# A two-layer attention and retention trunk: the order of the first supertile's queue, rotation and retention, the place of the output weights' squares, and the order of products in the first projection tiles

## The chip, the core and the metric

The kernel runs on one core of a Trainium2 chip. The core has five engines that each work through an instruction queue of their own, in order: TensorE (PE in the profile; its weight loads are listed apart as PEld), VectorE (DVE), ScalarE (ACT), GpSimd (POOL) and SyncE (SP), which issues the DMA transfers here. An instruction that needs another engine's result waits on a semaphore, and everything behind it in the same queue waits too. The metric is the device time of one execution, in microseconds (us).

## What is computed

Two layers, each `x <- x + W_out(concat[A(h) * silu(g_A), B(h) * silu(g_B)])` with `h = RMSNorm(x)`, then a last RMSNorm. There are 2048 tokens, a model width of 1024, 8 attention heads of 64 and 4 retention heads of 128. The core of the reference:

```python
proj = rms_norm(x, norm_gain[layer]) @ w_in
aq, ak, av, ag, rq, rk, rv, rg = jnp.split(proj, cuts, axis=-1)

# A: softmax attention over the own chunk of 64 and the 8 chunks before it
scores = einsum(qc, kb) * dh**-0.5 + rel_bias[clip(dist, -256, 256) + 256]
ya = softmax(where(valid, scores, -1e30)) @ vb

# B: retention; q and k are rotated by position, cos and sin of position * inv_freq
rotated = concat([t1 * c - t2 * s, t1 * s + t2 * c])
att     = einsum(qc, kc) * intra_decay
o_intra = att @ vc
state   = state * chunk_decay + kv          # from chunk to chunk
o_inter = einsum(qc, q_decay, state)
yr      = rms_norm(o_intra + o_inter)

x = x + concat([ya * silu(ag), yr * silu(rg)]) @ w_out
```

Everything is float32. The kernel gets there with fp16 matmuls: each factor is written as an upper half (`h`) and a rest (`l`), and a product is the sum of three matmuls, upper by upper, upper by rest and rest by upper.

## The kernel before, in words

**Tiling.** The kernel works by head pairs: in each layer `s` = 0 to 3 counts four pairs of attention heads with one retention head each, and each head pair runs over four supertiles `n` = 0 to 3 of 512 tokens. The normalized, transposed input of a supertile is `hTh` (upper) and `hTl` (rest), 8 blocks (`kt`) of 128 input channels, each with 512 tokens on the free axis. Tokens come in tiles of 128, numbered 0 to 15; supertile 0 holds tokens' tiles 0 to 3, supertile 1 holds 4 to 7.

**Projections.** `dense_T` (line 608) makes four tiles of a supertile, channels by tokens, each in 24 matmuls (8 blocks times 3 products): `j` = 0 is the attention's q, 1 its k, 2 the retention's q, 3 its k. The general loop stands at line 730; the very first supertile has its own, by token quarters, at line 712. `dense_V` (line 738) makes four tiles `a` = 0 to 3, tokens by channels, of 24 matmuls each at line 750: the columns are attention values, retention values and the gates. In both loops the three products of one block follow each other, block by block. The PSUM tiles come from a pool of two buffers (`psD`), so a tile can begin only when the one two before it has been read out. For V that reading ends on DVE in `rests` (lines 762 to 768), which is put off by one round; its three instructions write the rest of `v`, the rest of `rv` and the gate `gt`.

**Rounds.** A round is 8 matmuls of a projection. `run` advances the projection of the next supertile by a round, lets `attention` (line 783) of the supertile before take one of its 24 steps, runs what was put off with `later(k, f)` (f is issued k rounds on), and pulls a share of the background steps, which were handed over with `push(generator, steps)`. So TensorE's queue holds projection matmuls with attention and retention work between them. The instruction order within an engine is this order of issue where the code says so by hand, and the scheduler's elsewhere.

**Attention units.** A supertile has 8 units (4 tiles of 128 tokens, 2 heads), one in 3 rounds: scores S (lines 798, 799), bias and maximum on DVE (802), exp on ACT (805), the split into upper and rest (807 on ACT, 808 on POOL), a transposing DMA (810), the product with v (818 to 820) and its scaling on DVE (824 to 833).

**Retention.** `retention` (line 863) runs beside it: per token tile two steps, 8 in all. The first makes the scores r (products, line 853), their masking (872) and their split (`upper_of`, line 857, on ACT, and `rest_of`, line 861, on DVE, into a tile called dT in the profile). The second makes the output and the next state. DVE updates the state at lines 893 to 901, and lines 905 to 912 scale the output. The 8 steps are taken in rounds 0, 5, 6, 11, 12, 17, 18 and 23 of 24.

**Rotation.** For `j` = 2 and 3 `evacuate` (line 631) copies the tile out of PSUM as `raw`, `swap` exchanges its halves with two DMAs (line 666, into `swp`), and then follow, each some rounds on: `turn` (three POOL operations, lines 670 to 672, with the cosine and sine tables), `upper` (ACT, 675), `lower` (DVE, 678), for q `third` (ACT, 681) and for k `tokens` (a transposing DMA, 685).

**The first supertile.** Up to the end of its V tiles SP's queue has an order written by hand (`sp_order`), and the other engines get their work from a list of named steps. `x...4` to `x...7` are the steps of the next four token tiles: `sq` square, `rs` root, `mul` gain and scale, `hi` and `lo` the upper half and rest of the rows (token tile 7's stand on ACT and DVE), `dma` the two transposing DMAs into `hTh` and `hTl` (line 236). `bt` makes a bias tile from a table in memory: a POOL memset (580), a DMA (577), an ACT operation (581). `u` is one step of `tables` (line 83), which makes the cosine and sine tables of supertile 1 from its positions: it loads positions (`xa`, line 89), casts them on DVE (99), and goes on with DVE and ACT operations (93 to 124). The list that runs beside the last rounds is

```python
push(rounds(["xhi4 xrs5 xrs6", "xlo4 xmul5 xrs7", "xdma4 xhi5 xmul6 bt", "xlo5 xhi6 u", "xdma5 xlo6 xmul7",
             "xdma6 xhi7", "xlo7", "xdma7 u", "u u bt", "u u bt", "u u", "u u bt"]), 12)
```

`norms_from_input` (line 1148) does the same for later token tiles and loads their x itself; tiles 8 to 11 go into four spaces called `late`.

**Weights.** `convert` splits a head pair's weights into upper and rest: the rest of V's (`wlV`) is written on DVE (line 333). `prep_Omax` (line 492) takes the sum of squares of all of a layer's output weights, as their common scale needs it: 8 loads of 512 KB, 8 ACT squares (line 309) with DVE additions, and a sum over partitions. It is handed over as 13 steps in supertile 0 of `s` = 2, just before that supertile's V tiles. The bias tiles of a new head pair (`bt`) are made in supertile 0 as well.

## Time and profile before

| | |
|---|---|
| median of 3 runs | 2113.38 us (2111.25 to 2114.31) |
| the profiled execution's own time | 2117.65 us |
| its span | 2115.9 us |
| its mean granted TensorE clock | 0.987 |
| instructions | 39456 |
| HBM read, written | 123.26 MB, 41.98 MB |

The profile comes from one execution, and its span runs from the first to the last instruction that it recorded. A row of a group of instructions names the engine, the source line and the operands by the program's names (output<-inputs), the number, busy time and mean duration, and then the idle time of that engine just ahead of them with what ended it. A timeline row has the start (us from the span's beginning), the duration, the engine, the instruction, and in brackets the wait ahead of it with its releaser. Matmuls overlap in the records: their durations are longer than the distance between their starts. SPq rows are issues of DMAs, not their transfers.

### The profile page before, as it was taken

To read this page: it belongs to the slowest core of one execution; us is meant where nothing else is said; L and a number is where in the kernel's file an instruction comes from. 1 tells how busy PE (TensorE), PEld (TensorE's weight loads), DVE (VectorE), ACT (ScalarE), POOL (GpSimd) and SP (SyncE) were. 2 spreads that over 40 slices of the span, in tenths; PEclk is the share of its full clock that TensorE was granted. 3 is DMA by queue.
4 is the path that set the end of the run, shared out by engine and by line. 5 is a ranking of instruction groups with operands and counts; after the bars stand their busy time and mean duration, and the time that the engine had idled before them with its cause. 6 is when DMAs were issued, how large, how long until landed. Compare 5 with 4: busy or idle time off the path is not lost.

```text
span 2115.9 us, 39456 instructions
## 1 busy us (share of the span) xinstructions
PE 2010.4 (95%) x14014; PEld 1052.1 (50%) x14014; DVE 1253.8 (59%) x3839; ACT 1139.1 (54%) x2522; POOL 679.5 (32%) x701
## 2 busy tenths in 40 slices
PE   6778999999999999988999999999999999999998
PEld 4334555555455555544444555555545555554543
DVE  7677566655565655566653556555656566556643
ACT  7455665556655654555444546554665465446432
POOL 1233333433343433321002343434333433433200
PEclk9899999999999999999999999999999999999999
DMA  8767675558665764699875556555685567548874
GB/s 247 165 119 164 137 164 113 115 110 191 148 113 111 159 158 99 132 197 259 206 187 115 121 103 140 123 124 103 149 186 119 101 137 169 123 101 182 217 193 127
DMA packets 645701, 313.63 MB, mean 148 GB/s; under 512 B 459232, under 2 KB 602080, under 8 KB 645504
## 3 DMA queue, kind: packets, MB, share of 16 engines
q1 hardware_dynamic: 645504, 311.12, 66.5%
q8 instruction: 109, 1.79, 0.4%
q14 instruction: 88, 0.72, 0.1%
HBM read 123.26 MB, written 41.98 MB: 78 GB/s over the span
## 4 chain that ended last, share of the span: by engine, by line
PE 47%; DMA 3%; ACT 2%; DVE 2%; issue 1%; POOL 1%; SPq 1%; POOLq 0%; DVEq 0%; ACTq 0%
PE dT L730 14%; PE dV L750 14%; PE dO L1090 12%; DMA pT<-pq 2%; PE r L853 2%; PE S L799 1%; PE S L798 1%; PE o L818 1%; PE o L819 1%; PE o L820 1%; DVE sc L802 1%; ACT sc L805 0%; ACT pq L807 0%; DMA yhy<-rhy 0%; DMA bias<-toep 0%
## 5 line engine op out<-in xcount | busy, mean ns | idle before, releaser
L808 POOL TENSOR_TENSOR pq<-sc,pq 128x640 f16<-128x640 f32 (+4 forms) x256 | 319.9, 1250 | 930.1 <-ACT pq L807 562.5
L805 ACT ACTIVATE sc<-sc,mq,cT 128x640 f32<-128x640 f32 (+4 forms) x256 | 218.5, 853 | 653.8 <-DVE rl L824 330.4
L730 PE MATMUL dT<-hTh,whT 128*128 128x512 f16 x1008 | 386.0, 383 | 11.9 <-DVE rv L766 7.8
L750 PE MATMUL dV<-wlV,hTh 128*128 128x512 f16 x1024 | 389.1, 380 | 6.9 <-DVE wlV L333 6.9
L750 PE MATMUL dV<-whV,hTh 128*128 128x512 f16 x1024 | 389.3, 380 | 6.2 <-DVE gt L768 6.1
L730 PE MATMUL dT<-hTl,whT 128*128 128x512 f16 x1008 | 386.2, 383 | 4.6 <-DMA hTl<-hTl 2.9
L750 PE MATMUL dV<-whV,hTl 128*128 128x512 f16 x1024 | 389.0, 380 | 0.0
L730 PE MATMUL dT<-hTh,wlT 128*128 128x512 f16 x1008 | 385.7, 383 | 0.0
L730 PEld LDWEIGHTS <-whT 128*128 128x128 f16 x2016 | 195.9, 99 | 236.7 <-issue 20.4
L750 PEld LDWEIGHTS <-hTh 128*128 128x128 f16 x2048 | 197.7, 98 | 223.9 <-DVE gt L768 9.1
L802 DVE CUSTOM_DVE_ANT_0 sc<-S,bias 128x640 f32<-128x640 f32 (+4 forms) x256 | 188.8, 737 | 154.7 <-PE S L799 150.8
L1090 PE MATMUL dO<-whO,yhy 128*128 128x512 f16 x512 | 194.8, 381 | 1.9 <-DMA yhy<-rhy 1.9
L1090 PE MATMUL dO<-whO,yly 128*128 128x512 f16 x512 | 194.6, 380 | 0.8 <-DMA yly<-rly 0.8
L1090 PE MATMUL dO<-wlO,yhy 128*128 128x512 f16 x512 | 194.6, 380 | 0.0
L807 ACT ACTIVATE pq<-sc 128x640 f16<-128x640 f32 (+4 forms) x256 | 171.5, 670 | 11.1 <-DMA pT<-pq 3.0
L1090 PEld LDWEIGHTS <-yhy 128*128 128x128 f16 x1024 | 99.9, 98 | 117.2 <-DMA yhy<-rhy 2.6
L750 PEld LDWEIGHTS <-hTl 128*128 128x128 f16 x1024 | 100.3, 98 | 115.8 <-issue 9.9
L730 PEld LDWEIGHTS <-wlT 128*128 128x128 f16 x1008 | 99.3, 98 | 106.4 <-issue 4.3
L818 PE MATMUL o<-v,pT 128*128 128x65 f16 x1120 | 129.8, 193 | 15.6 <-DMA pT<-pq 15.5
L798 PE MATMUL S<-k,q 128*128 128x128 f16 (+3 forms) x592 | 142.3, 267 | 0.7 <-DVE mq L802 0.7
L818 PEld LDWEIGHTS <-pT 128*128 128x128 f16 x1120 | 105.7, 97 | 51.0 <-DMA pT<-pq 21.5
L819 PE MATMUL o<-v,pT 128*128 128x64 f16 x1120 | 130.0, 195 | 0.0
(350 smaller groups left out, 3499.3 us busy)
## 6 DMA issues: line engine op xcount, KB each, us to landing
q<-qq SPq DMA_DIRECT2D x128, 128.0 KB, 2.5
yyy<-y_d SPq DMA_DIRECT2D x32, 512.0 KB, 4.6
stT<-in_w_in_dram SPq DMA_DIRECT2D x27, 512.0 KB, 4.8
stV<-in_w_in_dram SPq DMA_DIRECT2D x26, 512.0 KB, 4.4
k<-kk SPq DMA_DIRECT2D x128, 64.0 KB, 2.1
swp<-rot SPq DMA_DIRECT2D x64, 128.0 KB, 2.6
tabc<-tab SPq DMA_DIRECT2D x32, 256.0 KB, 2.7
tabs<-tab SPq DMA_DIRECT2D x32, 256.0 KB, 3.1
```

The costliest lines, as they stand in the source:

```text
L730: pe.matmul(ps, w_[:, j, kt, :], h_[:, kt, :], start=(m == 0), stop=(m == 23))
L750: pe.matmul(ps, h_[:, kt, a * P:(a + 1) * P], w_[:, kt, :], start=(m == 0), stop=(m == 23))
L798: pe.matmul(o, st.q[:, hx, 0, cs], k_, start=True, stop=False)
L799: pe.matmul(o, st.q[:, hx, 1, cs], k_, start=False, stop=True)
L802: dve.tensor_tensor_reduce(out=v, in0=S[:, 0:w], in1=g.bias[hx][:, 640 - w:640], scale=1.0, scalar=-3.0e38, op0=ALU.add, op1=ALU.max, accu ...
L805: act.activation(v, v, AF.Exp, bias=m[:, 0:1], scale=g.c[:, 0:1])
L807: act.activation(pq[:, 0:w], v, AF.Copy)
L808: pool.tensor_tensor(pq[:, w:2 * w], v, pq[:, 0:w], op=ALU.subtract)
L818: pe.matmul(o[:, 0:65], u.p[:, b, :], v_[:, 0:65], start=(b == 0), stop=False)
L819: pe.matmul(o[:, 0:64], u.p[:, b, :], v_[:, 65:129], start=False, stop=False)
L853: pe.matmul(out_, w_, m_, start=(i == 0), stop=(i + 1 == len(pairs)))
L1090: pe.matmul(ps, h_[:, kt, :], w_[:, kt, :], start=(m == 0), stop=(m == 23))
```

## The change

Five edits:

1. `in_order`: in `dense_T` for `j` = 0 and in `dense_V` for `a` = 0 the 24 products are issued term by term (8 blocks of the first product, 8 of the second, 8 of the third). In the other tiles they stay block by block; in both, the order of the three products within a block or of the terms is changed (`hTl` last for T, `wlV`'s product last for V).
2. The first supertile's rotation: for q (`j` = 2) `upper`, `lower` and `third` go from rounds 6, 7, 8 after the evacuation to 11, 12, 13; for k (`j` = 3) `swap` goes from 5 to 9 rounds, while `turn`, `upper`, `lower` and `tokens` stand 3, 5, 6 and 7 rounds after it, as before.
3. The first supertile's retention takes its 8 steps in rounds 5, 10, 10, 14, 14, 18, 18 and 23.
4. The loads of x for token tiles 8 to 11 are steps `x8` of the hand-written list, behind `xdma7`, and `norms_from_input` leaves them out there; three of the `u` steps leave that list (7 in place of 10) and are pushed in the next supertile with the rest.
5. `prep_Omax` is handed over in supertile 2 of `s` = 2 in place of supertile 0, in both layers.

```diff
 
+    def in_order(apart, terms):
+
+        return [(kt, w) for w in terms for kt in range(KT)] if apart else [(kt, w) for kt in range(KT) for w in terms]
+
     def dense_T(l, s, n, g, st):
...
 
-                    d = 4 if j == 2 and first else 3
-                    later(d, turn)
-                    later(d + 2 if first else d + 3, upper)
-                    later(d + 3 if first else d + 4, lower)
-                    if j == 2:
-                        later(d + 4 if first else d + 6, third)
-                    if j == 3:
-                        later(7 if first else 11, tokens)
+                    if not first:
+                        plan = {3: turn, 6: upper, 7: lower, **({9: third} if j == 2 else {11: tokens})}
+                    elif j == 2:
+                        plan = {4: turn, 11: upper, 12: lower, 13: third}
+                    else:
+                        plan = {3: turn, 5: upper, 6: lower, 7: tokens}
+                    for k_, fn in plan.items():
+                        later(k_, fn)
 
...
                     st.rk = rot
-                    later(5 if first else 2, swap)
+                    later(9 if first else 2, swap)
 
...
             m = 0
-            for kt in range(KT):
-                for (w_, h_) in ((g.h, hh), (g.h, hl), (g.l, hh)):
-                    pe.matmul(ps, w_[:, j, kt, :], h_[:, kt, :], start=(m == 0), stop=(m == 23))
-                    m += 1
-                    if m in (8, 16) or (m == 24 and first):
-                        yield
+            for kt, (w_, h_) in in_order(j == 0, ((g.h, hh), (g.l, hh), (g.h, hl))):
+                pe.matmul(ps, w_[:, j, kt, :], h_[:, kt, :], start=(m == 0), stop=(m == 23))
+                m += 1
+                if m in (8, 16) or (m == 24 and first):
+                    yield
             evacuate(j, ps)
...
             m = 0
-            for kt in range(KT):
-                for (w_, h_) in ((g.vh, hh), (g.vl, hh), (g.vh, hl)):
-                    pe.matmul(ps, h_[:, kt, a * P:(a + 1) * P], w_[:, kt, :], start=(m == 0), stop=(m == 23))
-                    m += 1
-                    if m in (8, 16):
-                        yield
+            for kt, (w_, h_) in in_order(a == 0, ((g.vh, hh), (g.vh, hl), (g.vl, hh))):
+                pe.matmul(ps, h_[:, kt, a * P:(a + 1) * P], w_[:, kt, :], start=(m == 0), stop=(m == 23))
+                m += 1
+                if m in (8, 16):
+                    yield
             rv = gp.tile([P, 3, P], F16, tag="rv", name=f"rv{nm}_{a}")
...
         ret = retention(l, s, n, g, st)
+        rounds_ret = (5, 10, 10, 14, 14, 18, 18, 23) if (l, s, n) == (0, 0, 0) else [6 * a + b for a in range(4) for b in (0, 5)]
         for i, (a, hx) in enumerate(units):
...
             u = qk(a, hx)
-            if i % 2 == 0:
-                next(ret, None)
-            yield
-            yield
-            if i % 2 == 1:
-                next(ret, None)
-            pipe.append(lambda u=u: pv(u))
-            yield
+            for r in range(3 * i, 3 * i + 3):
+                for _ in range(rounds_ret.count(r)):
+                    next(ret, None)
+                if r % 3 == 2:
+                    pipe.append(lambda u=u: pv(u))
+                yield
 
...
             u.x = spaces[k] if spaces else w4.tile([P, D], F32, tag="w4", name=f"xin{u.t}")
-            sp.dma_start(u.x, x[u.t * P:(u.t + 1) * P, :])
+            if not spaces:
+                sp.dma_start(u.x, x[u.t * P:(u.t + 1) * P, :])
 
...
     t1 = tables(1, [xs0[1][:, i * 256:(i + 1) * 256] for i in range(4)])
-    steps = {"d": lambda: go_on(d0), "t": lambda: go_on(t0), "u": lambda: go_on(t1), "r": lambda: go_on(rl_),
+    x8 = (sp.dma_start(late[t - 8], x[t * P:(t + 1) * P, :]) for t in range(8, 12))
+    steps = {"x8": lambda: go_on(x8), "d": lambda: go_on(d0), "t": lambda: go_on(t0), "u": lambda: go_on(t1), "r": lambda: go_on(rl_),
              "Tu": T_un, "Vu": V_un, "bs": lambda: go_on(bs0), "bt": lambda: go_on(bt0)}
...
     g00.vdone = 4
-    push(rounds(["xhi4 xrs5 xrs6", "xlo4 xmul5 xrs7", "xdma4 xhi5 xmul6 bt", "xlo5 xhi6 u", "xdma5 xlo6 xmul7", "xdma6 xhi7",
-                 "xlo7", "xdma7 u", "u u bt", "u u bt", "u u", "u u bt"]), 12)
+    push(rounds(["xhi4 xrs5 xrs6", "xlo4 xmul5 xrs7", "xdma4 xhi5 xmul6 bt", "xlo5 xhi6", "xdma5 xlo6 xmul7", "xdma6 xhi7",
+                 "xlo7", "xdma7 x8", "u x8 bt", "u u x8 bt", "u u x8", "u u bt"]), 12)
     att = [None]
...
                     if n == 1:
-                        push(t1, TAB_STEPS - 10)
+                        push(t1, TAB_STEPS - 7)
                     push(norms_from_input(range(4 * n + 4, 4 * n + 8), late[0:4] if n == 1 else None,
...
                     push(wout_first(l, go, us), 10)
-                if n == 0 and s == 2:
+                if n == 2 and s == 2:
                     push(prep_Omax(l, go), 13)
```

## The prediction

> **What bounds the kernel now.** The page's first two parts come first: which engine is full, and where it is not.
>
> ```profile
> span 2115.9 us, 39456 instructions
> PE 2010.4 (95%) x14014; PEld 1052.1 (50%) x14014; DVE 1253.8 (59%) x3839; ACT 1139.1 (54%) x2522; POOL 679.5 (32%) x701
> PE   6778999999999999988999999999999999999998
> ```
>
> TensorE is busy for 2010.4 of 2115.9 us, and the holes stand in the first four slices (212 us). No matmul is added or removed, so the change can only touch the 105.5 us in which PE idles, and the half-speed stretches behind long idles. The view of waits, for PE alone, says what ended these idles (total, times, longest).
>
> ```profile
> PE r L853 <- DVE dT L861: 15.6, 10, 5.3
> PE r L853 <- ACT dT L857: 9.2, 3, 4.5
> PE dT L730 <- DVE rv L766: 7.8, 1, 7.8
> PE dV L750 <- DVE wlV L333: 6.9, 5, 1.6
> PE dT L730 <- DMA hTl<-hTl: 2.9, 1, 2.9
> PE dT L730 <- DMA hTl<-rln: 1.6, 2, 0.9
> ```
>
> Those six rows make 44 us, and each belongs to an edit. I take them by edit, the plainest first.
>
> **First tiles' products, term by term.** For V the first tile of four now multiplies whV by hTh eight times, whV by hTl eight times, and only then reads wlV; before, wlV was read by the second matmul.
>
> ```profile
> 506.00 0.38 PE L750 MATMUL dV<-wlV,hTh 128*128 128x512 f16 x1 [1.34 <-DVE wlV L333]
> 506.21 0.38 PE L750 MATMUL dV<-whV,hTl 128*128 128x512 f16 x1
> 506.43 0.38 PE L750 MATMUL dV<-whV,hTh 128*128 128x512 f16 x1
> ```
>
> Matmuls start 0.215 us apart. Sixteen before the first use of wlV instead of one add 15 x 0.215 = 3.2 us of cover, more than the longest of the five waits (1.6). The 6.9 us go, unless PE, 1.3 us earlier, meets the next wait sooner; the five reach from 1.3 to 1.6, so I leave 0.3 for that: **6.6**, bounds 4 (half of them come back) and 6.9.
>
> For the T tiles the same reordering puts hTl behind 16 matmuls on hTh. The two waits on hTl from the rln rows, 0.9 at the longest, are covered: **1.6**, bounds 0 and 3 (some half-clocked matmuls go with them).
>
> The Trainium skill, "TensorE: Matmul & The Clock Gate", section "Step-by-step: what each phase is for", speaks against such an order: weights are kept apart from the matmul so that one load can serve several matmuls, and the old order put the same weights twice in a row. In this trace nothing was kept: the page counts 14014 loads for 14014 matmuls, so by the row the order costs nothing; by the rule some of the T and V tiles' pairs would lose a load.
>
> **Squares of the output weights, two supertiles on.** `prep_Omax` leaves supertile 0 of the third head pair (s = 2) for supertile 2, in both layers: 8 loads of 512 KB, 8 squares with their accumulator reads, the additions, one matmul. Here are what the two places look like, ACT's squares, and the wait with its surroundings (ACT, then SP, then PE).
>
> ```profile
> 509.00:532.00 23.00, 22.70 (x163) 11.61 (x160) 11.51 (x40) 18.44 (x42) 11.69 (x11) 1.00 1.00 240
> 615.00:638.00 23.00, 23.00 (x173) 12.45 (x172) 15.00 (x46) 13.64 (x35) 11.33 (x12) 1.00 0.42 92
> L309 ACT ACTIVATE stO0m<-stO0m x8: 1039/1040/1056, 511.4 to 530.9; 128x1024 f32<-128x1024 f32 x8
> 534.63 0.83 ACT L581 ACTIVATE bias<-bias,ciT 128x640 f32<-128x640 f32 x1 [1.48 <-POOL bias L580]
> 527.15 1.63 SPq L577 DMA_DIRECT2D bias<-toep  x1
> 535.67 0.39 PE L853 MATMUL r<-rv,dT 128*128 128x128 f16 x2 [3.89 <-ACT dT L857]
> 536.36 0.59 PE L730 MATMUL dT<-hTh,whT 128*128 128x512 f16 x1
> 538.87 0.51 PE L730 MATMUL dT<-hTh,whT 128*128 128x512 f16 x1
> 1561.78 0.39 PE L853 MATMUL r<-rv,dT 128*128 128x128 f16 x2 [4.50 <-ACT dT L857]
> ```
>
> The columns of the first two rows are PE, PEld, DVE, ACT, POOL, clock, DMA share, GB/s. In supertile 0 ACT is busy 18.44 of 23 us, and the second bias tile, which only supertile 0 has, is issued by SP at 527.15, behind the eight loads that wait for squares to free their buffers. It lands so late that ACT's bias waits, and behind it in ACT's order stands the dT for which PE waits 3.89 (layer 0) and 4.50 us (layer 1). The six matmuls from 536.36 to 538.87 take 2.51 us instead of 6 x 0.215 = 1.29, so the idle costs 1.2 us more, about 1.5 with the small ones ahead of them; I put 2.0 on the longer idle of layer 1. Together 3.89 + 4.50 + 3.5 = 11.9.
>
> In supertile 2 ACT has 23 - 13.64 = 9.4 us free and no bias to wait for; 8 x 1.04 = 8.3 us of squares fit, with 1 us to spare. Its dT then comes late by little: I take 0.5 us per layer, so **10.9**. Bounds: 11.9, and 4 if ACT's order costs a wait there like the one removed, without its bias part. The loads there push the V weights' loads for the fourth head pair back, and SP waits on squares ahead of them; those weights are read a whole supertile (53 us) later, which covers it.
>
> **The first supertile's queue.** Before, SP held the eight transposes of tokens 4 to 7 behind the second rotation's swap. PE, then SP, POOL and ACT, then DVE:
>
> ```profile
> 76.35 0.58 PE L730 MATMUL dT<-hTh,whT 128*128 128x512 f16 x1 [7.78 <-DVE rv L766]
> 79.87 0.59 PE L730 MATMUL dT<-hTl,whT 128*128 128x512 f16 x1 [2.94 <-DMA hTl<-hTl]
> 59.89 0.56 SPq L577 DMA_DIRECT2D bias<-toep  x1
> 60.49 1.15 SPq L89 DMA_DIRECT2D xa<-in_pos_dram  x2
> 64.55 0.48 SPq L666 DMA_DIRECT2D swp<-raw  x1
> 72.92 1.30 SPq L236 DMA_TRANSPOSE hTh<-hTl  x1
> 63.25 1.27 POOL L672 TENSOR_TENSOR rot<-rot,swp 128x512 f32<-128x512 f32 x1
> 64.56 0.63 ACT L675 ACTIVATE rot<-rot 128x512 f16<-128x512 f32 x1 [4.85 <-POOL rot L672]
> 67.31 0.29 DVE L99 CAST xa<-xa 128x256 f32<-128x256 int32 x1
> 76.08 0.41 DVE L768 SCALAR_TENSOR_TENSOR gt<-gt,dV 128x256 f32<-128x256 f32 x1
> ```
>
> The swap waits for POOL's rotation to end (63.25 + 1.27), and six transposes stand behind it; the last hTh one is issued at 72.92 and lands as PE starts at 76.35. (The wait is put down to DVE's rv, but the DVE buffer this tile needs was free 7 us earlier.) ACT's upper half waits 4.85 us for the same rotation with token 7's rows behind it.
>
> Afterwards `upper` stands five rounds later, so ACT makes token 7's rows at once, and SP's order is bias, six transposes, one x load, two swaps, two position loads, x, x, bias, x. From 59.89 + 0.6: six transposes at 1.30 end at 68.3; token 7's hTh is issued at 65.7 and lands with the 3.4 us of 72.92 to 76.35 at about 69.2, its hTl at about 70.5. PE is ready at 68.4, so it waits 0.8 us instead of 7.8, and the 16 matmuls on hTh cover hTl.
>
> But the same move puts the position loads of the next tables, issued at 60.49 before, behind the transposes. Load 0.6, swaps 1.2 and positions 1.15 put their end at 68.3 + 0.6 + 1.2 + 1.15 = 71.3, and with the landing time of this row they arrive at 74.3:
>
> ```profile
> xa<-in_pos_dram SPq DMA_DIRECT2D x2, 64.0 KB, 3.1
> ```
>
> DVE's cast (67.31 before, not waiting) waits for them, and behind it in DVE's order stand six table operations, the first rotation's lower half and the last V tile's rests, which free the buffer of PE's second tile. In the old order these rests end at 76.5 (76.08 + 0.41), 9.2 us after the cast, of which about 4 are waits and operations that now stand elsewhere; 5.2 are left. So the second tile starts near 74.3 + 5.2 = 79.5, after 24 matmuls and an idle of 4.5 us.
>
> **Rotation and retention.** Retention's eight steps go from rounds 0, 5, 6, 11, 12, 17, 18, 23 to 5, 10, 10, 14, 14, 18, 18, 23: each result has 4 or 5 rounds after its scores and 4 instead of 6 after the state. All its operations stay; only POOL's bias memset, three table steps and the x loads change place beside them. DVE is what feeds all of it up to the next supertile's first tile, so I take the stretch by DVE's work. The window from the end of tile 2's rests (68.7) to its last state update (145.4), and its three largest idles there by releaser:
>
> ```profile
> 68.70:145.40 76.70, 54.57 (x295) 25.74 (x296) 52.10 (x136) 37.91 (x82) 24.23 (x29) 0.85 0.69 146
> L802 DVE CUSTOM_DVE_ANT_0 sc<-S,bias 128x128 f32<-128x128 f32 (+3 forms) x8 | 3.9, 484 | 6.1 <-PE S L799 6.1
> L764 DVE SCALAR_TENSOR_TENSOR v<-dV,v 128x128 f16<-128x128 f32 x5 | 1.4, 288 | 6.8 <-ACT rv L760 6.8
> L1168 DVE SCALAR_TENSOR_TENSOR hTh<-hTh,rsn,gb 128x1024 f32<-128x1024 f32 x2 | 2.6, 1283 | 3.4 <-POOL rsn L212 3.4
> 123.20 0.29 PE L853 MATMUL r<-rv,dT 128*128 128x128 f16 x1 [5.30 <-DVE dT L861]
> ```
>
> DVE works 52.10 us and idles 24.6. Now it starts at 74.3 with the same work, behind PE rather than ahead, so the 6.1 us for PE's scores go; ACT's rests (6.8, table loads among them) stay, and 3 of the rest. With 10 us of idle it ends at 74.3 + 52.1 + 10 = 136.4, and PE's next supertile starts **9.0** us earlier than before. A wait like that of 123.20 stays on the way, since DVE is later still against PE. Bounds: no idle at all gives 145.4 - 126.4 = 19.0; the old 24.6 gives 19.0 - 24.6 = -5.6, a loss.
>
> The clock after the 4.5 us idle is inside that, DVE being the limit. The Trainium skill's rule ("TensorE: Matmul & The Clock Gate", section "What's actually happening") halves the clock only after an idle window of some 3.4 us; the rows below show 0.61 us matmuls (0.38 at full speed) after two idles of 1.2 and 0.87. By the rule the 0.8 us left at 68.4 is harmless; by this row two such gaps close together cost about 1.5 us.
>
> ```profile
> 142.41 0.38 PE L730 MATMUL dT<-hTh,whT 128*128 128x512 f16 x1 [1.17 <-issue]
> 143.65 0.61 PE L730 MATMUL dT<-hTl,whT 128*128 128x512 f16 x1 [0.87 <-DMA hTl<-rln]
> ```
>
> The sum: 6.6 + 1.6 + 10.9 + 9.0 = 28.1 us. The profiled execution took 2117.65 us (span 2115.9 and 1.75 around it) and would take 2089.6; the runs' median, 4.3 lower, goes from 2113.38 to **2085**.
>
> **The rivals.**
> *The first supertile gives nothing* (20%): positions arrive later than 74.3, or DVE idles 19 us, and retention, now with 4 rounds of room, waits four times. For it: the old wait of 5.30, and 4.5 us of new PE idle. Against: PE's chain was bound by transposes, which do come earlier. 28.1 - 9.0 = 19.1, so 2094.
> *The first supertile gives all* (12%): DVE never idles. 28.1 + 10 = 38, so 2075.
> *The squares only move their wait* (6%): ACT's dT is late by 4 us in supertile 2, with the half clock behind it. Against: the 9.4 us free. 28.1 - 10.9 = 17.2, so 2096.
> *Slower* (5%): in the first supertile DVE, started 9 us late by the positions, falls so far behind that each retention step waits. The other edits give 19.1, so the turn comes where DVE idles more than 19.0 + 19.1 = 38 us, half as much again as the 24.6 now; at 45 us it is 2120.
> That SP's order is not what the change says can't be a rival: outside the first supertile the order is the scheduler's, and the built kernel's is as described.
>
> **How the numbers follow.** The forecast holds 57%. Its own range, from its bounds taken together, is 2078 to 2093. For 8 in 10 both first-supertile cases must be in, and above them the one in which the first supertile gives nothing and the squares move their wait as well (28.1 - 9.0 - 10.9 = 8.2, so 2105): 2075 to 2105. A measurement of this kernel can tell about 0.2% (4 us) from no change. Faster: 57 + 20 + 12 + 6 = 95, of which I give 3 to a rival reaching the edge: 0.92; same 0.03; slower 0.05.
>
> **What would show it.** In the new profile: no wait of dV on wlV; no wait of dT on hTl; no ACT dT wait of 4 us near the third head pair's start and at most 1 us two supertiles later; PE resuming near 69 us, then an idle near 75 to 80 us ended by DVE's rests, with DVE idle from 65 to 74 before the positions' cast. It is wrong if DVE does not idle there, if the second supertile's V ends later than 140 us, or if matmuls start further apart than 0.215 us: 28.1 us over some 6,100 projection matmuls is only 4.6 ns each.

## The result, and the profile after

The changed kernel takes 2092.59 us (median of 4 runs, 2087.95 to 2097.01), the kernel before 2113.85 us beside it: the ratio is 0.9898, 95% interval 0.9871 to 0.9924, so 21.3 us less. The profiled execution of it was its shortest, the profiled one of before its longest, so the two profiles lie further apart than the medians: spans of 2086.2 and 2115.9 us, 29.7 us. Here are the first parts of the page of the changed kernel (busy time by engine; PE's busy tenths in 40 slices).

```profile
span 2086.2 us, 39459 instructions
PE 2001.0 (96%) x14014; PEld 1047.6 (50%) x14014; DVE 1249.5 (60%) x3839; ACT 1137.9 (55%) x2522; POOL 677.7 (32%) x701
PE   6888999999999999988999999999999999999998
```

The matmuls are the same 14014; PE idles 85.2 us (2086.2 - 2001.0) where it idled 105.5, and its busy time fell by 9.4 us too. The matmuls being as many, this fits fewer of them at half speed (a granted clock of 0.5, called half clock here): the mean granted clock is 0.995 over the span, and was 0.987. The view of PE's waits in the changed kernel (total, times, longest):

```profile
PE o L820 <- DMA pT<-pq: 13.2, 15, 1.9
PE r L854 <- DVE dT L862: 10.0, 12, 3.8
PE r L854 <- DVE sh L862: 7.1, 5, 4.4
PE dV L752 <- DVE gt L770: 6.9, 5, 1.6
PE dT L733 <- DVE gt L770: 5.0, 1, 5.0
PE r L854 <- ACT dT L858: 4.5, 3, 1.8
```

Of the six rows that the prediction named, those of wlV, of hTl (two) and of rv are gone altogether, ACT's dT fell from 9.2 to 4.5, DVE's dT from 15.6 to 10.0. New are 5.0 us of T on gt, and sh rose from 1.8 to 7.1.

Where the time came from is best read by laying the two timelines side by side: the start of the first matmul of the same tile, before minus after. The same was done for three kernels that hold one part of the change each (the first three experiments below) and for a second profile of the changed kernel (the fourth). A step down a column is gained or lost in the stretch between two rows. Supertiles are numbered from 0 as in the code (the expectations below count from the one behind the first: their second supertile starts at 142.41 before and 139.4 in the changed kernel, their third at 209.01).

| tile, and its start before (us) | changed | changed again | order alone | squares alone | first supertile alone |
|---|---|---|---|---|---|
| supertile 1, first T tile, 76.35 | 6.09 | 6.01 | -0.68 | -0.47 | 6.60 |
| supertile 1, second T tile, 87.69 | 6.97 | 5.02 | 2.29 | 0.04 | 5.34 |
| supertile 2, first T tile, 142.41 | 2.99 | 1.24 | 2.55 | 0.31 | 1.12 |
| supertile 2, second T tile, 151.13 | 5.46 | 3.71 | 5.02 | -1.15 | 0.87 |
| supertile 3, first T tile, 209.01 | 5.47 | 3.99 | 5.15 | -0.64 | 1.07 |
| supertile 3, second T tile, 219.83 | 7.24 | 6.00 | 5.88 | 0.13 | 1.04 |
| next head pair (s = 1), first V tile, 296.89 | 7.25 | 6.00 | 5.87 | 0.12 | 1.03 |
| s = 1, second V tile, 304.97 | 8.97 | 7.73 | 7.59 | -1.52 | 1.03 |
| s = 2, second V tile, 512.13 | 10.30 | 8.80 | 9.07 | -0.80 | 1.74 |
| s = 2, supertile 1, second T tile, 543.62 | 16.31 | 14.80 | 6.64 | 5.21 | 0.65 |
| s = 2, T tile after the squares' new place, 650.98 | 13.28 | 11.68 | 6.64 | 1.79 | 0.65 |
| layer 1, s = 2, first V tile, 1530.83 | 20.33 | 19.23 | 12.99 | 3.80 | 4.27 |
| layer 1, s = 2, supertile 1, second T tile, 1570.34 | 27.99 | 26.90 | 11.96 | 11.09 | 3.99 |
| layer 1, s = 2, T tile after the new place, 1677.69 | 25.43 | 24.37 | 11.96 | 8.43 | 3.99 |
| whole span, 2115.9 | 29.7 | 25.4 | 15.0 | 10.0 | 5.9 |

A column holds one execution, and the same stretch does not come out alike each time. The edits of experiments 4, 6 and 11 leave the first supertile as the changed kernel has it, and their supertile 2 starts later than the 139.41 of the first profile. PE's timelines of experiments 4, 6 and 11:

```profile
141.17 1.89 PE L733 MATMUL dT<-hTh,whT 128*128 128x512 f16 x8 [1.22 <-issue]
141.18 1.89 PE L733 MATMUL dT<-hTh,whT 128*128 128x512 f16 x8 [1.22 <-issue]
141.38 2.92 PE L733 MATMUL dT<-hTh,whT 128*128 128x512 f16 x8 [1.13 <-issue]
```

So at that row the change gives 3.0 us in one profile and 1.0 to 1.2 in three, and a difference of less than 2 us there is not told from chance. Behind it too a column moves without an edit: the kernel with the squares alone by 1.5 us to the next row (0.31 to -1.15).

**V's order.** The first V tile of the third head pair in the changed kernel (PE's timeline):

```profile
495.48 1.89 PE L752 MATMUL dV<-whV,hTh 128*128 128x512 f16 x8
498.38 1.89 PE L752 MATMUL dV<-whV,hTl 128*128 128x512 f16 x8
500.10 1.89 PE L752 MATMUL dV<-wlV,hTh 128*128 128x512 f16 x8
501.83 0.38 PE L752 MATMUL dV<-whV,hTh 128*128 128x512 f16 x1
```

No wait stands in front of wlV's eight, and the tile behind starts on time. The same holds at all five places: 1.5 us gained at four of them and 1.7 at the first.

**T's order.** Supertile 3's first tile, PE's timeline, first before, then changed:

```profile
209.01 0.58 PE L730 MATMUL dT<-hTh,whT 128*128 128x512 f16 x1 [2.98 <-DMA hTh<-rhn]
210.35 0.61 PE L730 MATMUL dT<-hTl,whT 128*128 128x512 f16 x1 [0.76 <-DMA hTl<-rln]
...
212.89 0.63 PE L730 MATMUL dT<-hTl,whT 128*128 128x512 f16 x1
```

```profile
203.53 3.42 PE L733 MATMUL dT<-hTh,whT 128*128 128x512 f16 x8 [2.97 <-DMA hTh<-rhn]
...
207.97 1.89 PE L733 MATMUL dT<-hTh,wlT 128*128 128x512 f16 x8
```

The wait of 2.97 us for hTh is the same in both, and half clock follows in both. Before, a second wait of 0.76 stood a few matmuls on, and six matmuls later PE was still at 0.63 us apiece (0.38 at full clock); afterwards the eight after 207.97 take 1.89 together. The step in the table is 7.24 - 5.47 = 1.77 us here and 5.46 - 2.99 = 2.47 in supertile 2.

**Squares.** The old place is clean (no wait of PE on ACT's dT is left there). The new one, PE, ACT and DVE of the changed kernel:

```profile
622.85 0.28 PE L854 MATMUL r<-rv,dT 128*128 128x128 f16 x2 [1.26 <-ACT dT L858]
623.71 0.23 PE L854 MATMUL r<-rv,dT 128*128 128x128 f16 x1 [0.41 <-DVE dT L862]
620.35 1.06 ACT L309 ACTIVATE stO0m<-stO0m 128x1024 f32<-128x1024 f32 x1
622.54 0.26 ACT L858 ACTIVATE dT<-r 128x128 f16<-128x128 f32 x1
619.82 0.42 DVE L506 TENSOR_TENSOR omaxO<-omaxO,m1O0m 128x1 f32<-128x1 f32 x1 [2.80 <-ACT stO0m L309]
621.36 0.29 DVE L873 TENSOR_TENSOR r<-r,msk 128x128 f32<-128x128 f32 x1
```

Two queues are late together. On ACT the eighth square (620.35) stands ahead of the evacuation and of dT. On DVE the running sum of the squares (line 506) waits 2.80 us for the seventh square, and the mask of retention's scores (line 873), from which ACT's dT is made, stands behind it. The table shows 16.31 - 13.28 = 3.0 us given back in layer 0 and 27.99 - 25.43 = 2.6 in layer 1.

**First supertile.** PE, then DVE and SP of the changed kernel:

```profile
65.07 0.39 PE L752 MATMUL dV<-whV,hTh 128*128 128x512 f16 x1 [1.58 <-DVE gt L770]
70.26 1.89 PE L733 MATMUL dT<-hTh,whT 128*128 128x512 f16 x8
80.72 0.61 PE L733 MATMUL dT<-hTh,whT 128*128 128x512 f16 x1 [5.01 <-DVE gt L770]
107.79 0.28 PE L854 MATMUL r<-rv,dT 128*128 128x128 f16 x2 [1.78 <-ACT dT L858]
112.60 0.27 PE L854 MATMUL r<-sh,rot 128*128 128x128 f16 x1 [4.42 <-DVE sh L862]
74.74 0.69 DVE L99 CAST xa<-xa 128x256 f32<-128x256 int32 x1 [7.38 <-DMA xa<-in_pos_dram]
69.85 1.25 SPq L89 DMA_DIRECT2D xa<-in_pos_dram  x2
```

Tokens 4 to 7 are transposed in time, so the first T tile starts 6 us earlier and without a wait; the positions come at 74.7, DVE idles 7.4 us for them, and PE waits 5.0 for the second tile's buffer. After that the retention waits 1.8 and 4.4 us in the middle of the supertile, and of the lead of 7.0 us 3.0 are left at its end (in the profile taken again 5.0 and 1.2).

### The profile page after: what moved, and what is told of

The parts are those of the page before. It is cut to its first block, busy times and chain, and to the rows that moved or that the text cites. A ratio compares the mean times of both kernels' runs of the same rounds, so it can differ in the third digit from the quotient of the medians.

```text
span 2086.2 us, 39459 instructions
## 1 busy us (share of the span) xinstructions
PE 2001.0 (96%) x14014; PEld 1047.6 (50%) x14014; DVE 1249.5 (60%) x3839; ACT 1137.9 (55%) x2522; POOL 677.7 (32%) x701
## 3 DMA queue, kind: packets, MB, share of 16 engines
q8 instruction: 109, 1.79, 0.4%
## 4 chain that ended last, share of the span: by engine, by line
PE 47%; DMA 4%; ACT 2%; DVE 2%; issue 1%; POOL 1%; SPq 1%; POOLq 0%; DVEq 0%; ACTq 0%
PE dT L733 14%; PE dV L752 13%; PE dO L1091 13%; DMA pT<-pq 2%; PE r L854 2%; PE S L800 1%; PE S L801 1%; PE o L820 1%; PE o L821 1%; PE o L822 1%; DMA toep<-rel_d 1%; ACT sc L807 0%; DVE sc L804 0%; ACT pq L809 0%; DMA yhy<-rhy 0%
## 5 line engine op out<-in xcount | busy, mean ns | idle before, releaser
L752 PE MATMUL dV<-whV,hTh 128*128 128x512 f16 x1024 | 352.9, 380 | 7.1 <-DVE gt L770 6.9
L733 PE MATMUL dT<-hTh,whT 128*128 128x512 f16 x1008 | 348.8, 381 | 9.1 <-DVE gt L770 5.0
L752 PE MATMUL dV<-whV,hTl 128*128 128x512 f16 x1024 | 352.9, 380 | 0.0
L752 PE MATMUL dV<-wlV,hTh 128*128 128x512 f16 x1024 | 352.5, 380 | 0.0
L733 PE MATMUL dT<-hTh,wlT 128*128 128x512 f16 x1008 | 347.1, 379 | 0.0
L733 PE MATMUL dT<-hTl,whT 128*128 128x512 f16 x1008 | 347.1, 379 | 0.0
L800 PE MATMUL S<-k,q 128*128 128x128 f16 (+3 forms) x592 | 142.2, 266 | 0.7 <-DVE mq L804 0.7
L820 PEld LDWEIGHTS <-pT 128*128 128x128 f16 x1120 | 105.5, 97 | 50.2 <-DMA pT<-pq 21.9
```

The lines of the kernel that those rows point to most:

```text
L733: pe.matmul(ps, w_[:, j, kt, :], h_[:, kt, :], start=(m == 0), stop=(m == 23))
L752: pe.matmul(ps, h_[:, kt, a * P:(a + 1) * P], w_[:, kt, :], start=(m == 0), stop=(m == 23))
L800: pe.matmul(o, st.q[:, hx, 0, cs], k_, start=True, stop=False)
L820: pe.matmul(o[:, 0:65], u.p[:, b, :], v_[:, 0:65], start=(b == 0), stop=False)
```

## The experiments

Each is timed against the kernel before on one chip, the first four together, the next four, the last four.

**1. Order alone.** The kernel before with

```diff
+    for kt, (w_, h_) in in_order(j == 0, ((g.h, hh), (g.l, hh), (g.h, hl))):     # dense_T
...
+    for kt, (w_, h_) in in_order(a == 0, ((g.vh, hh), (g.vh, hl), (g.vl, hh))):  # dense_V
```

> The kernel before, with the order of the products alone (edit 1). Theory: the five waits of V on wlV go (about 6.3 us) and the two waits of T on hTl go with the half-clocked matmuls behind them (1.8 us at the third supertile's start, up to 2.5 at the second's): 8 to 11 us faster, and no other row changes. Rival: the 2.5 us at the second supertile's start come from the first supertile's edits and not from the order: 8 us or less. Rival against: TensorE meets the next wait sooner and gives half of V's back: 5 us.

2102.67 us against 2114.33, ratio 0.9939 (0.9927 to 0.9951): 11.7 us, more than half of the whole. T brings 2.55 us up to supertile 2's start, then 2.47 and 0.73; so the T steps at 151 and 220 belong to the order and not to the first supertile's edits, which alone show nothing there (0.87 and 1.04 after 1.12 and 1.07). The step of 0.73 alone would prove little: the squares alone show 0.77 there without the order. V's five steps stand as in the changed kernel. At the squares its column falls by 2.4 (9.07 to 6.64): PE comes there earlier, waits 4.4 us for ACT's dT in place of 3.9, and half clock lasts 6.8 us there in place of 3.4.

**2. Squares alone.**

```diff
-                if n == 0 and s == 2:
+                if n == 2 and s == 2:
```

> The kernel before, with the squares of the output weights two supertiles on alone (edit 5). Theory: the waits of 3.9 and 4.5 us and their half clock go, and in supertile 2 new waits of 1.3 (ACT) and about 1 us stand, some 3 us given back per layer: 5 to 9 us faster. Rival (the forecast): 0.5 us given back per layer, 10.9 faster. Rival: the new waits in supertile 2 come only together with the other edits, and then nothing is given back here.

2107.68 us, ratio 0.9963 (0.9951 to 0.9976): 6.7 us by the medians. The old place gives 5.21 + 0.56 = 5.8 us in layer 0 (from the fourth V tile's start, where its lead was -0.56) and 11.09 - 3.80 = 7.3 in layer 1; the new place takes back 3.4 and 2.7. The new waits come with this edit alone, so the last rival falls, and the forecast of 0.5 us per layer with it.

**3. First supertile alone.**

```diff
+                        plan = {4: turn, 11: upper, 12: lower, 13: third}
...
+                    later(9 if first else 2, swap)
...
+        rounds_ret = (5, 10, 10, 14, 14, 18, 18, 23) if (l, s, n) == (0, 0, 0) else ...
...
+                 "xlo7", "xdma7 x8", "u x8 bt", "u u x8 bt", "u u x8", "u u bt"]), 12)
```

> The kernel before, with the first supertile's queue, rotation and retention alone (edits 2 to 4). Theory: the second tile's wait (5 us) and DVE's late start give back what the earlier transposes bring, and the second supertile's first matmul starts 3 us earlier than before: 2 to 4 us faster. Rival (the forecast): 9 us. Rival: the edit needs the term-by-term order, because hTl lands late in the first tile; without it a wait of 1 to 3 us and half clock stand there, and the gain is nothing.

2111.78 us, ratio 0.9993 (0.9983 to 1.0003): 2.5 us by the medians, and an interval that includes no change at all. In the traces 1.1 us are left at supertile 2's start. So these edits, the longest part of the diff, bring the least. The third expectation is seen in small only: hTl is waited for in the first tile, by 0.80 us.

**4. The changed kernel again**, unchanged, beside the three.

> The changed kernel once more, beside the single edits on one chip. If the three edits add, its gain is the sum of theirs within 3 us, 20 to 22 us by the medians. If the granted clock is what makes its runs differ, the spans of its runs follow the clock: 0.001 of clock is about 2.1 us, and its profile shows a half-clock stretch of 3.4 us behind other idles than the last profile, for the same waits.

2092.71 us, ratio 0.9896 (0.9883 to 0.991): 21.6 us. The sum of the three medians is 11.7 + 6.7 + 2.5 = 20.9, so they add. The four runs of the changed kernel shown first took 2087.95 at a mean clock of 0.995, 2092.61 and 2092.56 at 0.993 and 0.992, and 2097.01 at 0.991: 9.1 us over 0.004, 2.3 us per 0.001. The four of this experiment do not keep to it: 2090.01 at 0.994, 2092.23 at 0.992, 2096.47 at 0.991, but 2093.19 at 0.995. The expectation that the clock makes the runs differ is therefore not borne out as it stands. The second profile does show half clock where the first has none (from 934.70 and from 962.01, 3.4 us each); with the waits ahead of them PE falls some 2 us further behind the first profile at each, and has made this up by 985.

**5. Early positions.** The changed kernel with the position loads back ahead of the last transposes:

```diff
-"xlo5 xhi6", ... "xdma7 x8", "u x8 bt", ...
+"xlo5 xhi6 u", ... "xdma7 x8", "x8 bt", ...
```

> The changed kernel with one step moved: the position loads of the next tables stand ahead of the last token tiles' transposes, where they stood before the change, and all else as changed. Theory (DVE, started late by the positions, is the limit of the first stretch): DVE no longer idles 7.4 us ahead of its cast, the second tile's wait of 5 us goes to under 1, and the second supertile's first matmul starts 4 to 7 us earlier than the changed kernel's 139.4. Rival (retention's four rounds are the limit): the waits at 106 to 113 us (6.2 us in all) grow by what DVE gains, and 0 to 2 us are left. Rival: the last transposes, 1.3 us later, leave an idle of 2 to 3 us before the first tile, and half clock takes the gain.

2092.72 us, ratio 0.9903 (0.9885 to 0.9921), the changed kernel's within what can be told. The second tile starts at 75.9 and not 80.7, as the theory said, but the gain is gone a tile later. PE, then POOL:

```profile
83.36 0.28 PE L854 MATMUL r<-rot,rot 128*128 128x128 f16 x2 [2.04 <-ACT rot L679]
85.56 0.58 PE L733 MATMUL dT<-hTh,whT 128*128 128x512 f16 x1 [1.11 <-DVE qq L638]
76.45 1.26 POOL L674 TENSOR_TENSOR raw<-raw,tabc 128x512 f32<-128x512 f32 x1 [11.77 <-DMA swp<-raw]
```

The wait only moved: retention's first scores in round 5 now wait for the rotated k, whose swap landed at 76.3, and with 0.51 and 1.11 us more behind it PE idles 3.7 us in all and falls to half clock. None of the three had named this wait. Supertile 2 starts at 139.41: as in the changed kernel's first profile, and 1.8 us before the three others that have its first supertile. Of the 4 to 7 us expected, 0 to 2 are there.

**6. Squares spread over the whole supertile.** The changed kernel with the hand-over ahead of T's rounds:

```diff
+                if n == 2 and s == 2:
+                    push(prep_Omax(l, go), 13)
                 if not first:
                     run(dT, att, ...)
...
-                if n == 2 and s == 2:
-                    push(prep_Omax(l, go), 13)
```

> The changed kernel with the squares handed over at the start of supertile 2 and not at its V tiles, so that 13 steps go over 24 rounds and not 12. Theory (the squares stand too close for ACT, and dT of the retention comes late behind them): the waits of 1.3 and 1.5 us on ACT's dT and what follows them in supertile 2 go, 2 to 3 us per layer, 4 to 6 in all. Rival: the place is no better, a square stands ahead of another dT, and the time stays within 2 us.

2109.02 us, ratio 0.9984 (0.9971 to 0.9996): 16 us slower than the changed kernel, against both expectations. ACT's groups over the stretch (with the idle before them), then PE:

```profile
L309 ACT ACTIVATE stO0m<-stO0m 128x1024 f32<-128x1024 f32 x8 | 8.4, 1051 | 8.1 <-DMA stO0m<-in_w_out_dram 8.1
603.09 0.39 PE L854 MATMUL r<-rv,dT 128*128 128x128 f16 x2 [4.35 <-ACT dT L858]
```

In T's rounds SP also issues the transfers of q, k and the swaps, the squares' loads are issued between them, and ACT waits 8.1 us for loads with retention's dT behind the waiting square. In the place of the change ACT has no such wait. How close the squares stand matters less than whether each one's load is there when its turn comes.

**7. Five rounds between states.** The changed kernel with

```diff
-rounds_ret = (5, 10, 10, 14, 14, 18, 18, 23)
+rounds_ret = (5, 9, 9, 14, 14, 19, 19, 23)
```

> The changed kernel with the first supertile's retention in rounds 5, 9, 9, 14, 14, 19, 19, 23: five rounds between one state and its next use and not four. Theory (four rounds are too few for state, upper half and rest): the wait of 4.4 us on the rest of sh at 112.6 shrinks by about a round, 2 us, with half the half clock behind it, and the second supertile starts 1 to 4 us earlier. Rival (DVE is late as such): the same wait stands a round later, and nothing changes within 1 us. Rival: the first output, now four rounds behind its scores, waits for its dT in round 9: slower by 1 to 2.

2095.15 us, ratio 0.991 (0.9895 to 0.9925). The wait on sh is 3.2 us, against 4.4 in the changed kernel's first profile but 3.3 to 3.5 in the three others with its first supertile, so the edit is not shown to shrink it. A later wait of V on gt is 3.2 us and 1.5 in all four of those. Supertile 2 starts at 140.86, inside their 139.41 to 141.38. What more room at one step gives, if anything, is not seen at the end.

**8. Early positions and five rounds.**

> The last two edits (early positions, five rounds) together. If DVE's start and the rounds are two separate limits, the second supertile starts earlier by the sum of what each gives alone; if the one hides the other, by 3 us or more beyond the sum; if DVE's start is all, by what the early positions give alone.

2091.67 us, ratio 0.9902 (0.9883 to 0.992). Supertile 2 starts at 138.53, 0.9 us earlier than in the changed kernel's first profile and 2.6 to 2.9 earlier than in the three others. Against the first, the two alone gave 0 and -1.5 us, so that they would ease each other by 2.4; against the others they gave 1.8 to 2.0 and 0.3 to 0.5, which about adds up. With that spread neither is shown; in time it can't be told from the changed kernel.

**9. Retention from round 7.** Early positions, and

```diff
+rounds_ret = (7, 11, 11, 15, 15, 19, 19, 23)
```

> The kernel with early positions, and the first supertile's retention in rounds 7, 11, 11, 15, 15, 19, 19, 23. With early positions alone TensorE waited 3.7 us at 81 to 85 for the rotated k in round 5, and half clock followed. Theory (the rotation of k ends about 83 us and retention's first step was too early for it): with the first step two rounds later no idle over 1 us stands between 76 and 90 us, no half clock there, and the second supertile starts 3 to 5 us earlier than with early positions alone (139.4). Rival (DVE and the four rounds of the later steps are the limit): the wait on the rest of sh, 4.7 us at 112, grows, and the start stays within 1 us.

2093.59 us, ratio 0.99 (0.988 to 0.9921). The wait for the rotated k is gone, but the start of supertile 2 is 143.56, 2.2 to 4.2 us later than in the four profiles with the changed first supertile: a wait of 6.95 us on ACT's dT stands at 131.7. A miss of the theory; what that wait is shows in experiment 12. Part of the delay has another source: in this execution the first T tile itself starts at 72.84 and not near 70.3, behind 3.58 us of waiting for hTh's transposes.

**10. Loads of x behind the swap.** Early positions, and

```diff
-"xdma7 x8", "x8 bt", "u u x8 bt", "u u x8", "u u bt"
+"xdma7", "bt", "u u x8 bt", "u u x8 x8", "u u x8 bt"
```

> The kernel with early positions, and the four 512 KB loads of x moved behind the rotation's swap. With early positions the swap, issued at 70.6, landed at 76.4 behind the first load. Theory (the load ahead of the swap makes k's rotation late): the swap lands 2 to 3 us earlier, POOL's rotation ends near 78, the 2.0 us wait for the rotated k in round 5 goes under 1 us, and the second supertile starts 1 to 3 us earlier than 139.4. Rival (ACT's queue, where the exp and the bias stand ahead of k's upper half, sets it): the wait stays, 0 to 1 us.

2090.32 us, ratio 0.9882 (0.9867 to 0.9896), the lowest median of all, though its interval overlaps the changed kernel's. POOL, then PE:

```profile
73.10 1.26 POOL L674 TENSOR_TENSOR raw<-raw,tabc 128x512 f32<-128x512 f32 x1 [8.01 <-DMA swp<-raw]
82.25 0.38 PE L733 MATMUL dT<-hTh,whT 128*128 128x512 f16 x1 [0.69 <-DVE qq L638]
135.29 3.15 PE L733 MATMUL dT<-hTh,whT 128*128 128x512 f16 x8 [1.32 <-issue]
```

The swap, issued at 69.9 in place of 70.6, lands at 72.9 in place of 76.3: without the 512 KB load ahead of it, it took 3.0 us and not 5.7. The wait for the rotated k and the half clock are gone, and supertile 2 starts at 135.3, 4.1 us before the earliest profile of the changed first supertile (139.4) and so clear of its spread, more than was expected. By supertile 3's second T tile 2.7 of these are left (9.93 in the table's measure, against 7.24).

**11. Seven squares.** The changed kernel with the last square and its load left out:

```diff
-        for j in range(KT):
+        for j in range(KT - 1):
...
-            if j + 1 < KT:
+            if j + 1 < KT - 1:
...
-        for _ in range(4):
+        for _ in range(5):
```

> The changed kernel with the last of the eight squares of the output weights and its load left out (the scale of the output weights is then taken from seven eighths of them). Theory (the eighth square stands on ACT just ahead of the evacuation and of retention's dT): the wait of 1.3 us on ACT's dT in supertile 2 of the third head pair, 1.5 in layer 1, goes under 0.3, and of the 3.0 and 2.6 us given back there 1.5 to 2 come back in each layer. Rival (ACT is full there whatever the last square does): the seventh takes its place and the wait stays over 1 us.

2092.24 us, ratio 0.9889 (0.9872 to 0.9905). PE, DVE and ACT at the squares' new place:

```profile
625.94 0.28 PE L854 MATMUL r<-rv,dT 128*128 128x128 f16 x2 [0.61 <-DVE rss L906]
627.25 0.23 PE L854 MATMUL r<-rv,dT 128*128 128x128 f16 x1 [0.85 <-DVE dT L862]
623.57 0.42 DVE L506 TENSOR_TENSOR omaxO<-omaxO,m1O0m 128x1 f32<-128x1 f32 x1 [2.80 <-ACT stO0m L309]
625.61 0.28 ACT L858 ACTIVATE dT<-r 128x128 f16<-128x128 f32 x1 [0.47 <-DVE r L873]
```

The theory missed; of the rival the number held and not its reason. Without the last square ACT is early, waits 0.47 us itself, and PE still waits 1.46 us (1.67 with it): now on DVE, where the sum waits the same 2.80 us for the seventh square, with the mask and dT's rest behind it. Only 0.9 of the 3.0 us came back in layer 0 and 0.4 of 2.6 in layer 1. So the last square's share on ACT is the smaller part of what is given back. That the greater part runs through DVE's sum is read from these rows and not tested: a sum issued a round later, or once at the end, would have shown it, and wasn't tried.

**12. Loads of x behind the swap, and retention from round 7.**

> Early positions, the loads of x behind the swap, and retention in rounds 7, 11, 11, 15, 15, 19, 19, 23, together. If round and swap are two ways of easing the same wait for the rotated k, the second supertile starts as with the better of the two, within 1 us; if they are separate, by the sum.

2091.35 us, ratio 0.9888 (0.9873 to 0.9903). Supertile 2 starts at 138.35, later than with experiment 10 alone. PE, then ACT:

```profile
127.17 0.39 PE L854 MATMUL r<-rv,dT 128*128 128x128 f16 x2 [7.20 <-ACT dT L858]
121.91 1.28 ACT L121 ACT_TABLE_LOAD   x1
124.10 1.28 ACT L761 ACT_TABLE_LOAD   x1
126.86 0.26 ACT L858 ACTIVATE dT<-r 128x128 f16<-128x128 f32 x1
```

A round later retention's dT falls behind the sine step of the tables, for which ACT changes its function table twice, 1.28 us each time. This is the 6.95 us wait of experiment 9 too. With the rounds of the change dT runs ahead of that step (in the first profile dT at 123.82, the first table load at 125.11); with all of them shifted it doesn't.

## Why the prediction was right, and where it was not

The direction and the range held: 2085 forecast, 2092.6 measured, inside 2075 to 2105. But the terms were off on both sides, T's order too small and the squares and the first supertile too large, and the time is nearest to the rival in which the first supertile gives nothing (2094). The errors partly cancel: T's order brought 2.6 us more than forecast, the three others 9.4 less. The range, 30 us wide, would have held without that; that it is met says little for the sizes of the terms.

| term | forecast | measured, from the table's steps | changed again |
|---|---|---|---|
| V order | 6.6 | 6.3: five steps of 1.5 to 1.7, less 1.4 that later waits took back | 6.0 |
| T order | 1.6 | 4.2: 2.47 + 1.77 | 4.5 |
| squares | 10.9 | 7.8: (16.31 - 10.54) + (27.99 - 20.33) gained, 3.0 + 2.6 given back | 7.8 |
| first supertile | 9.0 | 3.0 at supertile 2's start | 1.2 |
| sum | 28.1 | 21.3 | 19.5 |

(That 21.3 is also the difference of the medians is chance, as the last column shows. 10.54 is the lead at the start of the fourth V tile of s = 2 in layer 0 (525.42 before), behind the gain of V's order.) The first two profiles differ by 8.4 us more than this sum, as the profiled runs lie 3.8 us over one median (2117.65 - 2113.85) and 4.6 under the other (2092.59 - 2087.95). That part stands where no edit is, at waits of o on pT and around the output projections: about 2 us each at 1003, 1520 and 1735 us before, and 1.25 in the last projection. At the first two, half clock followed a wait in the profile of before and none in that of after; the order alone and the first supertile alone show the same steps there.

**V's order** went as worked out: 16 matmuls of cover, no wait on wlV, a part taken back by the next wait (0.53 us behind the first of the five, where o waits 0.36 for pT).

**T's order** was mis-sized: the waits on hTl were counted by their own length (1.6 us) with "some half-clocked matmuls" in the upper bound of 3 alone. They stand a few matmuls behind other idles, and in the profile of before half clock lasted there for a stretch more than in that of the changed kernel (3.4 us against none at 143, 6.8 against 3.4 at 208). So 0.87 us of waiting came to 2.47, and 0.76 to 1.77. The size is not firm: over the eleven profiles that hold the order the two steps are 0.8 to 2.5 and 0.7 to 2.0 us, and in the order alone half clock lasted 6.8 us at supertile 3 although the wait on hTl was gone. The Trainium skill's rule on keeping weights for several matmuls ("TensorE: Matmul & The Clock Gate", section "Step-by-step: what each phase is for") took nothing back: the loads are 14014 as before, and matmuls start 0.215 us apart in either order (501.83, then 502.05 and 502.26).

**Squares.** The wait removed was sized well: 5.77 + 7.66 = 13.4 us against 11.9, half clock included. What failed is the step that priced the new place by ACT's free time (9.4 us free, 8.3 needed, so 0.5 us late per layer). Over the whole stretch ACT was less full than reckoned:

```profile
601.00:624.00 23.00, 21.21 (x163) 11.21 (x162) 12.32 (x47) 18.40 (x45) 9.02 (x8) 1.00 0.92 224
```

(columns as before: ACT is the fourth, 18.40 of 23 us.) Room over the stretch was not what decided, but the order on two queues. On ACT, exp, split, two squares and the evacuation follow each other from 617.06 to 622.8 almost without a pause, with dT at their end. On DVE the sum waits for the square behind that exp and split, and retention's mask waits behind the sum. Experiment 11 shows that the wait on DVE remains when ACT is relieved of the last square. The rival that squares move their wait was right in kind, at 2.8 us a layer and not 4 with half clock behind it.

**First supertile.** The forecast's steps came nearly as written: the last hTh landed at 68.55 (forecast 69.2), PE went on at 70.3 behind a late V tile, the cast at 74.7 (74.3), the second tile at 80.7 after 5.0 us of idle (79.5 after 4.5). What failed is the step that gave DVE 10 us of idle time from there to the next supertile. The window from the cast to the last state update:

```profile
74.74:142.19 67.45, 51.50 (x295) 24.14 (x294) 51.48 (x138) 36.59 (x78) 24.02 (x27) 0.92 0.58 131
L766 DVE SCALAR_TENSOR_TENSOR v<-dV,v 128x128 f16<-128x128 f32 x5 | 1.4, 287 | 6.2 <-ACT rv L762 6.2
L231 DVE TENSOR_TENSOR rln<-hTh,rhn 128x1024 f16<-128x1024 f32 x2 | 2.8, 1402 | 3.2 <-DMA pT<-pq 1.9 <-DMA hTl<-rln 1.3
```

DVE's work was right (51.48 us against 52.10), but it idles 16.0 us (67.45 - 51.48): the 6.2 for rv stay, and 3.2 for transposes on SP's queue are new. 74.7 + 51.5 + 16.0 = 142.2 in place of 136.4, 5.8 us, which is the miss of 9.0 against 3.0. In the three other profiles with this first supertile the positions' cast came later as well, at 76.4 to 76.8, with 13.9 to 14.2 us of idle behind it; their last state update ends at 143.8 to 144.1. And little of the 3.0 belongs to these edits: the order alone has 2.55 at the same row, the edits alone 1.1. "DVE is what feeds all of it" was too simple as well: with the position wait taken away (experiment 5) DVE starts 8.6 us earlier, at 66.2, and supertile 2 starts 0 to 2 us earlier, because the rotated k, set by SP's queue and the swap's landing, comes next. With that removed too (experiment 10) 7.1 of the forecast 9.0 us stand at 142.41.

The 1.58 us wait at 65.07 was not foreseen. Tokens 4 to 7 had landed before PE came (68.55 for the last hTh), so the first T tile would have started earlier without it; nothing is lost by it, since the second tile waits for DVE's rests until 80.7 in any case.

Of the signs named ahead, one failed: ACT's dT was to wait at most 1 us two supertiles on, and PE waited 1.26 us for it in layer 0 and 1.48 in layer 1. And of the six rows that were each given to an edit, the largest, DVE's dT, kept 10.0 of its 15.6 us.

## What to carry to other kernels

A short wait can be worth more than its length where it follows another: sum the idles of the last few us before pricing it, since half clock may hold the matmuls behind. Before a step of 1 or 2 us in one profile is read as an effect, look at what the same stretch does in a second profile of the same code. A helper step that is moved for one engine's sake must be checked on every in-order queue it touches: here the square fitted on ACT, while its sum on DVE and its load on SP (in experiment 6) held up what stood behind them. And a long reordering of a start-up phase, where five queues wait for each other in turn, gives back most of each wait that it removes; the two edits that only move a product or a hand-over brought 18.4 of the 21 us (11.7 + 6.7).

## What the runs showed of the hardware

When half clock follows an idle of PE is sharper than the prediction had it, and not certain in between. Over all 14 profiles of this study, taking idles that stand alone (no other within 5 us, after the first 60 us), a half-clock stretch of 3.4 us or a multiple of it began behind 1 of 256 idles of 0.25 to 1.88 us, behind 9 of 23 from there to 2.6 us, and behind all 30 longer ones. Two of the middle kind from the kernel before, each with the window behind it (the clock is the number after the five engines):

```profile
1517.81 0.20 PE L818 MATMUL o<-v,pT 128*128 128x65 f16 x1 [2.27 <-DMA pT<-pq]
1734.15 0.20 PE L818 MATMUL o<-v,pT 128*128 128x65 f16 x1 [2.33 <-DMA pT<-pq]
...
1518.75:1522.10 3.35, 3.35 (x16) 1.54 (x14) 1.64 (x8) 1.76 (x5) 0.00 (x0) 0.50 0.90 177
1734.00:1737.40 3.40, 3.25 (x35) 2.06 (x36) 1.64 (x8) 0.86 (x1) 0.00 (x0) 1.00 0.90 183
```

The shorter of the two was followed by half clock, the longer not. By the clock of 0.50 in a stretch of 3.4 us, each costs an estimated 1.7 us of matmul time, where nothing behind it takes that up. Idles of the middle size that stand alone come once or twice in a profile. Whether this is why runs of one kernel differ by 9 us stays open. The two profiles of the changed kernel (spans 2086.2 and 2090.5) speak against it: what stays of their 4.3 us came in the first supertile (1.1) and at waits of o on pT that were longer in the second (1.81 us against 0.31 near 1708, 1.58 against 0.38 near 1905), with no half clock behind them. The Trainium skill puts half clock behind at least one idle window of some 3.4 us, and says that the window runs freely, so that its place against the work decides ("TensorE: Matmul & The Clock Gate", section "What's actually happening"). The second half agrees with these runs, where the same length goes either way and the stretches are of 3.4 us or multiples; the first doesn't, since an idle of 1.9 us can be enough.
